# Relative-position bias rows made among the first chunks, 32 copies in DRAM instead of 128, and each Toeplitz tile loaded in four parts

## The chip, the cores and the metric

One core of a Trainium2 chip runs the whole program in one launch. The metric is the device time of that core in microseconds, the median of several runs. A core has five engines that work through their own instruction lists in order and wait for each other by semaphores: TensorE (PE, the matrix products; PEld is its weight load), VectorE (DVE), ScalarE (ACT), GpSimd (POOL) and SyncE (SP). DMA transfers are issued from the lists of SP and of ACT here and carried out by 16 DMA engines.

## The reference

Two transformer blocks on 512 positions of width 1024, in float32. The first block mixes a gated short convolution, a causal attention of 8 heads of 64 with a relative-position bias (with two key blocks of 256 every visible key is taken, so it is plain causal attention), and an attention over 256 memory rows, then a feed-forward part. The second block has an index-based sparse attention, a gated linear recurrence, a memory attention and a feed-forward part. The change lies in the bias of the first block's causal attention:

```
def moba_attention(q, k, v, rel_bias):      # rel_bias: (32 buckets, 8 heads)
    ...
    bias_hb = rel_bias.astype(jnp.float32).T
    ...
        dist = t[:, None] - (own * MOBA_BLOCK + blk_off)[None, :]
        bias_own = bias_hb[:, rel_bucket(dist)]
        s_own = jnp.where(dist[None, None] >= 0, s_own + bias_own[None], NEG)
```

The bias of a head depends on the distance between query and key alone, so one row of 640 numbers per head holds it, with a large negative number where the key lies ahead of the query.

## The kernel before, in words

Every product is made of three float32r products of high and low parts (`passes`, L175 to L177), so each weight tile of 512 KB is loaded by SP (`load`, L187), cast to its high part by ACT (L197) and subtracted to its low part by DVE (L198) ahead of its use. A class `Program` holds the products in the order of TensorE as jobs. Background work is written as Python generators that advance some steps at each tick of the jobs; all of this only sets the order in which instructions stand in each engine's list when the program is built. Nothing is reordered later: an engine that waits holds up all that stands behind it in its list.

The first part of the program runs so. `begin` loads the input, norms the first token tiles, and issues small constant loads from ACT's list (L501 to L503). `head_chunks` makes the first four chunks (q0, k0, q1, k1 of the attention's query and key projections, 128 features each), first for the first 256 positions, then, as half 1, for the other 256; hooks can be put ahead of a (half, chunk). `use_q` and `use_k` copy a finished chunk into operand tiles (`stack_q` L540 and L542, `stack_k` L547 to L551). Then `gemm_N` makes the values v (four weight tiles, copied out at L756). Then come the twelve chunks of the convolution with the remaining q and k chunks between them, and the gate products of the first branch.

The bias is prepared by the generator `bias_rows`, started after the head chunks and driven by the ticks of the v product: it loads a 33x640 one-hot table and the bias table, multiplies them on TensorE (L524, two column parts), copies the 8x640 result from PSUM (L525), and writes each head's row 128 times to a DRAM tile `rdram` [8, 128, 640] (L526). `toeplitz(hd)` then loads a 128x512 tile (L531) from `rdram` with a row step of 639, so that each partition gets the row shifted by one.

```
        nc.scalar.dma_start(rdram, rrow[:, None, :].to_broadcast([8, P, 640]))
        ...
        nc.scalar.dma_start(t, bass.AP(tensor=base.tensor, offset=base.offset + P - 1, ap=[[639, P], [1, 512]]))
```

The attention is the generator `chain(*(moba_pair(c) for c in range(4)))`, at 0.35 step per tick, beside the convolution chunks and the first gates. A pair of heads begins with its two `toeplitz` loads; then `causal_pair` makes the scores of four row blocks i = 3, 2, 1, 0 (`stacked`, L554 and L555); DVE adds the Toeplitz tile and takes the row maximum (L586); ACT makes the exponentials (L588) and, after a reciprocal on DVE (L594), scales them (L597); TensorE transposes them (L307) and multiplies with the values (L614). PSUM has 8 banks (`bank()`), which are taken in turn, so a product can wait for the reader of a bank's former content. The framework also takes the completion semaphores of all DMAs from a small set in turn: a DMA is not issued before the former transfer on its semaphore has landed, whichever list that one was issued from.

Of the kernel before, what the change touches and what calls it, by code (L numbers as in the profile page):

```python
# [28 lines left out]
# columns of the packed per-channel vectors  # L29
# [9 lines left out]
class Program:  # L39
    """The matrix products in the order of the tensor engine, each with the weight tiles it needs.  # L40

    Weight tiles are loaded and split ahead of their use; background work (generators) advances by
    some steps after each product, so that what it waits for is done under the products."""
# [39 lines left out]
    def fetch(self, n):  # L83
        """loads up to n tiles more than are split"""
        while len(self.loaded) < min(len(self.flat), len(self.got) + n):
            self.loaded.append(self.load(self.flat[len(self.loaded)][0]))

    def prepare(self):
        """splits the next tile"""
        self.fetch(1)  # L90
        n = len(self.got)
        kind, on_pool = self.flat[n][1:]
        self.got.append(self.split(self.loaded[n], kind != "w", on_pool))
        self.loaded[n] = None
        self.held += kind == "w"
# [48 lines left out]
def body(tc, ctx, io):  # L144
# [58 lines left out]
    # ---- constants  # L203
# [17 lines left out]
    def rsqrt_small(n, parts, scale, post=None):  # L221
        """(sum * scale + eps) ** -0.5 of [P, n] sums of squares (scale 1 for two partial means)"""
        ms, rs = small(n), small(n)
        if len(parts) == 2:
            g_.tensor_scalar(ms, parts[0], parts[1], EPS, op0=ALU.add, op1=ALU.add)
        else:
            g_.tensor_scalar(ms, parts[0], scale, EPS, op0=ALU.mult, op1=ALU.add)
        g_.tensor_tensor(out=rs, in0=ms, in1=negh[:, :n], op=ALU.pow)  # L228
        if post is not None:
            r2 = small(n)  # L230
            pool_scale(r2, rs, post)
            rs = r2
        return rs
# [6 lines left out]
    class Act:  # L240
        """A [K, tokens] operand, split in two float32r parts, as pairs of 128-row chunks."""
# [16 lines left out]
        def put_pairs(self, j, t, ps, gain=None):  # L258
            """ps: [128, 512] with token tile t of two pairs"""
            parts = []  # L260
            for i in range(2):
                self.alloc(j + i)
                cols = slice(t * P, (t + 1) * P)
                parts.append((self.h[j + i][:, :, cols], self.l[j + i][:, :, cols],
                              ps[:, i * 256:(i + 1) * 256].rearrange("p (k t) -> p k t", k=2)))
            for hi, lo, x in parts:
                if gain is None:
                    a_.copy(hi, x)  # L268
                else:
                    a_.activation(hi, x, AF.Copy, scale=gain)  # L270
            for hi, lo, x in parts:
                if gain is None:
                    sub_lo(lo, x, hi)
                else:
                    v_.scalar_tensor_tensor(lo, x, gain, hi.bitcast(F32), op0=ALU.mult, op1=ALU.subtract)  # L275
# [5 lines left out]
    class Chunks:  # L281
        """A [K, tokens] operand whose 128-row chunks come one by one."""
# [28 lines left out]
    # ---- norms of token tiles  # L311
    def norm_y(x, sq, gain):
        """x: [P, D] of one token tile; sq: its two partial mean squares"""
        rs = rsqrt_small(1, sq, 1.0)
        y = slot([P, D])
        for hf in range(2):
            c = slice(hf * 512, hf * 512 + 512)
            v_.scalar_tensor_tensor(y[:, c], x[:, c], rs, gain[:, c], op0=ALU.mult, op1=ALU.mult)
        return y
# [10 lines left out]
    # ---- products  # L330
    def gemm_T(w, x, out, nk=KD, cols=(0, 512)):
        """out[:, cols] = (weights [nk*128, 128])^T x, in parts; w = (hi, lo) tiles, [k, m] in a row."""
        hi, lo = w
        c0, c1 = cols
        for k in range(nk):
            s = slice(k * P, (k + 1) * P)
            passes(out[:, c0:c1], hi[:, s], lo[:, s], x.hi(k)[:, c0:c1], x.lo(k)[:, c0:c1], k == 0, k == nk - 1)
            if k % 2 and k < nk - 1:
                yield

    def chunk(src, x, use, **kw):
        """job: one 128-feature chunk, feature-major; use(psum)"""
        def f(w):
            o = bank()
            yield from gemm_T(w, x(), o, **kw)
            use(o)
        pr.job(f, [src])

    def head_chunks(srcs, x, uses, before):
        """first chunks of a phase, the first two token tiles ahead of the others;  # L350
        before: hooks {(half, chunk): fn}"""
# [24 lines left out]
    def gemm_N(srcs, x, use, nt=NT):  # L376
        """jobs: a token-major product with one 512-column block; use(t, psum)"""
# [26 lines left out]
    def gemm_out(src, npair, x, epi0, epi1, res=4, korder=None, late=None, need={}):  # L404
        """jobs: [tokens, 1024] = x^T W; src(half, pair) -> DRAM tile; epilogues per token tile.
        late(t) is queued two tiles after epi1(t)."""
# [49 lines left out]
    # ---- the first norm  # L456
# [21 lines left out]
    def begin():  # L478
# [21 lines left out]
        first_norm(2)  # L500
        nc.scalar.dma_start(vecs, io["c_vecs"])  # L501
# [9 lines left out]
    # ---- block 1: relative position bias, as one row per head in DRAM  # L511
    rdram = drp.tile([8, P, 640], F32, name="rdram")

    def bias_rows():
        oneh = slot([33, 640])
        nc.scalar.dma_start(oneh, io["c_onehot"])
        rb = cst.tile([33, 8], F32, name="rb")
        g_.memset(rb[32:33, :], 1.0)
        nc.scalar.dma_start(rb[0:32, :], io["rel_bias"])
        yield from wait(4)  # L520
        rrow = slot([8, 640])
        for c0, c1 in ((0, 512), (512, 640)):
            ps = bank()
            mm(ps[:8, :c1 - c0], rb, oneh[:, c0:c1], start=True, stop=True)  # L524
            v_.tensor_copy(rrow[:, c0:c1], ps[:8, :c1 - c0])  # L525
        nc.scalar.dma_start(rdram, rrow[:, None, :].to_broadcast([8, P, 640]))  # L526

    def toeplitz(hd):
        t = tmp()
        base = rdram[hd]  # L530
        nc.scalar.dma_start(t, bass.AP(tensor=base.tensor, offset=base.offset + P - 1, ap=[[639, P], [1, 512]]))  # L531
        return t

    # ---- attention
    HALVES = ((slice(0, 64), slice(64, 128)), (slice(64, 128), slice(0, 64)))

    def stack_q(dst, ps, scale=1.0):
        """dst: per head [128, n]: the float32r parts of 64 rows, one above the other"""
# [5 lines left out]
    def stack_k(dst, ps):  # L544
        """dst: per head two [128, n]: each of the two parts of 64 rows, twice"""
# [11 lines left out]
    def p_view(sl, s, i):  # L557
        """columns of the triangle's row block i (i + 1 key blocks)"""
# [8 lines left out]
    def causal_pair(ops, vh, addm, put, ready=None):  # L567
        """two heads of 64; ops(s) = stacked (q, kh, kl) of [128, 512]; vh(s, j): [128, 64];
        addm(s, i): [128, (i+1)*128] to add to the scores; put(psum [128, 512])"""
# [47 lines left out]
    def mem_heads(heads, scale, put, parts=False):  # L617
        """heads: (score(t, out), v(j), first row, rows) over 256 memory rows; put(psum [128, 512]);
        v(j) may be the pair of the values' parts"""
# [48 lines left out]
    class MemT:  # L668
        """the normed memory rows, feature-major and split"""
# [35 lines left out]
    # ---- block 1: mixing  # L705
# [52 lines left out]
    def moba_pair(c):  # L758
        def g():
            while ("kl", c) not in qk:  # L760
# [10 lines left out]
                {(0, 1): small_consts, (0, 3): lambda: late_T(2), (1, 0): lambda: late_T(3)})  # L771
    pr.start("bias", bias_rows)
    gemm_N([io["w_in_v"][j] for j in range(4)], H, use_v)
    pr.drain("bias")
# [87 lines left out]
    # ---- norm after a branch, residual, norm before the next one  # L862
    def post_norm(gpost, gpre, half):
        """half: a power of two that the branch's values lack"""
# [35 lines left out]
    def next_head(late, srcs, uses, after=None):  # L900
        """the next phase's first chunks, with the last two tiles' transposes among them"""
# [8 lines left out]
    # ---- block 1: feed forward  # L910
# [32 lines left out]
    # ---- block 2: index scores and the top 128 keys of each query  # L943
# [80 lines left out]
    # ---- block 2: memory attention  # L1024
    def head_norm(ps, nq, nk):
        """ps: [P, (nq + nk) * 64] token-major; rms over 64; the nk last heads come twice each"""
# [20 lines left out]
    def stack_qT(q, t, y, gain):  # L1047
        """the parts of y's four heads of 64, transposed, to q's token tile t"""
# [46 lines left out]
    class Heads:  # L1095
        """four heads' [128, n], in two slots"""
# [47 lines left out]
    # ---- block 2: HGRN2  # L1144
    hg = {}

    def silu2(out, ps):
        """twice silu: x * (1 + tanh(x / 2))"""
# [57 lines left out]
    def hgrn_offsets(j):  # L1206
        """sums of whole 64-chunks between a position's chunk and the level's reference point, of two heads"""
# [16 lines left out]
    class Level:  # L1224
        """one level of one head, in three steps on three engines and the products"""
# [200 lines left out]
    # ---- block 2: the order of the mixing's products  # L1426
# [35 lines left out]
    # ---- block 2: output projection, residual, feed forward  # L1462
# [63 lines left out]
# ---- host side: layouts only  # L1526
def _pack_t(w):
    """[K, M] -> one tile [128 k, (k chunks) 128 m] for each 128 columns"""
# [4 lines left out]
def _pack_n(w, perm=None):  # L1533
    """[K, M] -> tiles [128 k, 2 k chunks, 512 m], the 512-column blocks outermost"""
# [8 lines left out]
def _cols(v):  # L1543
    """[n*128] -> [128, n]"""
    return v.reshape(-1, P).T
# [93 lines left out]
```

## Time and profile before

| what | value |
|---|---|
| time, median of 3 runs | 1602.97 us (1602.64 to 1603.36) |
| profiled execution, first to last instruction | 1605.4 us |
| TensorE busy | 1525.8 us, 95% |
| VectorE, ScalarE, GpSimd busy | 49%, 37%, 15% |
| mean granted TensorE clock | 0.973 |
| DMA, bytes moved | 153.80 MB, mean 96 GB/s |

The page gives for each engine the busy time as a share of the span. The granted clock is told per stretch of time, with 1.00 for full speed. Views by stretch give the busy microseconds of each engine inside it, so the length of the stretch minus PE's busy time is the time in which TensorE had nothing to run. A line of the timeline tells start, duration, engine, line of the program and operation, and in brackets how long the engine was idle before it and what ended the wait; the letter q after an engine's name marks an instruction of its list that only issues a DMA.

### The profile page before, as it was taken

The page shows a single profiled execution, that of the slowest core. Times are in us where ns is not written, and L with a number is a line of the kernel's source. Part 1 is how long each engine was busy: PE and PEld are TensorE (multiplying, and loading weights), DVE is VectorE, ACT ScalarE, POOL GpSimd, SP SyncE. Part 2 cuts the span into 40 slices and gives each one's busy share as a digit, 9 for nine tenths or more (in the row PEclk, how much of TensorE's full clock was granted, in tenths as well). Part 3 has the DMA queues.
Part 4 walks back from the last instruction along what each step waited for, and adds up shares of the span by engine and source line. Part 5 has one row for each costly group of instructions (what it writes and reads, how often), then busy time and mean ns, then how long its engine had stood idle before and what let it go on. Part 6 is the DMA issues. An engine that isn't in the chain of part 4 may idle for free.

```text
span 1605.4 us, 20374 instructions
## 1 busy us (share of the span) xinstructions
PE 1525.8 (95%) x8107; PEld 1265.8 (79%) x8107; DVE 790.3 (49%) x1200; ACT 597.4 (37%) x1043; POOL 238.3 (15%) x344
## 2 busy tenths in 40 slices
PE   8929999999999999999999998999789999999999
PEld 7727788888888888888888986767568988888887
DVE  5215545455345566666324478988744333333231
ACT  5214545344334333333223465465533222222120
POOL 1000000012111100000000167725320000000000
PEclk9959999999999999999999999999799999999999
DMA  5432223332234033223334222221221132232331
GB/s 179 100 62 90 88 90 117 126 98 79 93 112 157 28 104 105 93 92 105 106 118 136 95 89 84 92 72 54 93 79 66 66 103 95 93 104 92 105 118 53
DMA packets 46437, 153.80 MB, mean 96 GB/s; under 512 B 5092, under 2 KB 5604, under 8 KB 46342
## 3 DMA queue, kind: packets, MB, share of 16 engines
q1 hardware_dynamic: 41472, 142.62, 26.9%
q10 hardware_dynamic: 4870, 9.87, 2.8%
q8 instruction: 64, 1.05, 0.3%
q14 instruction: 31, 0.25, 0.0%
HBM read 145.66 MB, written 6.82 MB: 95 GB/s over the span
## 4 chain that ended last, share of the span: by engine, by line
PE 79%; DVE 7%; ACT 4%; POOL 3%; issue 2%; another core or an unknown queue 2%; DMA 1%; SPq 0%; DVEq 0%; POOLq 0%; ACTq 0%
PE p L175 25%; PE p L176 25%; PE p L177 25%; PE p L307 2%; ACT s L588 1%; DVE s L1006 1%; DVE s L1272 1%; POOL m L228 1%; DVE m L1005 1%; ACT t L237 1%; PE p L614 1%; ACT s L597 1%; DVE s L180 0%; POOL s L183 0%
## 5 line engine op out<-in xcount | busy, mean ns | idle before, releaser
L175 PE MATMUL p<-s,wh 128*128 128x512 f32 (+1 forms) x1192 | 465.6, 391 | 0.9 <-DVE t L1312 0.6
L176 PE MATMUL p<-s,wh 128*128 128x512 f32 (+1 forms) x1192 | 462.9, 388 | 0.0
L177 PE MATMUL p<-s,wl 128*128 128x512 f32 (+1 forms) x1192 | 462.5, 388 | 0.0
L198 DVE TENSOR_TENSOR wl<-r,wh 128x1024 fp32r<-128x1024 f32 x217 | 258.3, 1192 | 329.9 <-ACT wh L197 329.0
L197 ACT CAST wh<-r 128x1024 fp32r<-128x1024 f32 x233 | 232.9, 1001 | 232.6 <-PE p L176 220.5
L175 PEld LDWEIGHTS p<-s,wh 128*128 128x128 f32 x1192 | 225.0, 189 | 46.7 <-DVE t L1312 0.8
L177 PEld LDWEIGHTS p<-s,wl 128*128 128x128 f32 x1192 | 225.0, 189 | 45.8
L176 PEld LDWEIGHTS p<-s,wh 128*128 128x128 f32 x1192 | 225.0, 189 | 44.0
L175 PE MATMUL p<-wh,s 128*128 128x512 f32 x544 | 218.5, 402 | 4.4 <-ACT s L270 4.4
L177 PE MATMUL p<-wh,s 128*128 128x512 f32 x544 | 215.0, 395 | 1.1 <-DVE s L275 0.6
L176 PE MATMUL p<-wl,s 128*128 128x512 f32 x544 | 214.6, 394 | 0.0
L176 PE MATMUL p<-s,s 128*128 128x256 f32 (+1 forms) x408 | 132.7, 325 | 5.6 <-DVE s L180 5.6
L175 PE MATMUL p<-s,s 128*128 128x256 f32 (+1 forms) x408 | 133.5, 327 | 0.5 <-ACT s L268 0.5
L177 PE MATMUL p<-s,s 128*128 128x256 f32 (+1 forms) x408 | 132.2, 324 | 0.0
L183 POOL TENSOR_SCALAR s<-t 128x512 fp32r<-128x512 f32 (+1 forms) x64 | 34.7, 543 | 655.7 <-DVE t L930 223.4
L175 PEld LDWEIGHTS p<-wh,s 128*128 128x128 f32 x544 | 103.8, 191 | 26.6 <-ACT s L270 4.8
L177 PEld LDWEIGHTS p<-wh,s 128*128 128x128 f32 x544 | 103.6, 191 | 24.1 <-DVE s L275 1.0
L176 PEld LDWEIGHTS p<-wl,s 128*128 128x128 f32 x544 | 103.9, 191 | 20.2
L176 PEld LDWEIGHTS p<-s,s 128*128 128x128 f32 x408 | 79.9, 196 | 11.9 <-DVE s L180 6.6
L175 PEld LDWEIGHTS p<-s,s 128*128 128x128 f32 x408 | 80.0, 196 | 6.5 <-ACT s L268 1.2
L177 PEld LDWEIGHTS p<-s,s 128*128 128x128 f32 x408 | 79.9, 196 | 5.3
L307 PE MATMUL p<-ident,s 128*128 128x128 f32 x400 | 60.1, 291 | 16.4 <-ACT s L597 6.3
(182 smaller groups left out, 1420.2 us busy)
## 6 DMA issues: line engine op xcount, KB each, us to landing
r<-w_up SPq DMA_DIRECT2D x44, 512.0 KB, 3.4
r<-w_ffn_in SPq DMA_DIRECT2D x44, 512.0 KB, 3.3
r<-w_in_gate SPq DMA_DIRECT2D x24, 512.0 KB, 3.3
r<-w_down SPq DMA_DIRECT2D x22, 512.0 KB, 3.3
r<-w_ffn_out SPq DMA_DIRECT2D x22, 512.0 KB, 3.3
r<-w_out SPq DMA_DIRECT2D x16, 512.0 KB, 3.3
r<-w_in_conv SPq DMA_DIRECT2D x12, 512.0 KB, 3.3
r<-w_in_qk SPq DMA_DIRECT2D x8, 512.0 KB, 3.7
```

Source lines behind the costliest of these rows:

```text
L175: mm(out, sh, mh, start=start, stop=False)
L176: mm(out, sh, ml, start=False, stop=False)
L177: mm(out, sl, mh, start=False, stop=stop)
L183: g_.tensor_scalar(out, x, s, 0.0, op0=ALU.mult, op1=ALU.add)
L197: a_.copy(hi[:, :n], raw)
L198: (g_ if on_pool else v_).tensor_tensor(out=lo[:, :n], in0=raw, in1=hi[:, :n].bitcast(F32), op=ALU.subtract)
L228: g_.tensor_tensor(out=rs, in0=ms, in1=negh[:, :n], op=ALU.pow)
L237: a_.activation(tmp(), x, AF.Square, scale=scale, accum_out=acc)
L307: pe.transpose(ps[:m, n:n + P], s, ident)
L588: a_.activation(pv, pv, AF.Exp, scale=-1.0, bias=negm[s][:, i:i + 1], accum_out=sums[s][:, i:i + 1])
L597: a_.activation(pv, pv, AF.Copy, scale=rec[s][:, i:i + 1])
L614: mm(ps[64 * s:64 * s + 64, j * P:512], vh(s, j), p_view(PT, s, 3 - j), start=(j == 0), stop=(j == 3))
```

## The change

The bias table and one-hot loads go to a new function `bias_load`, called in `begin` ahead of the three constant loads. `bias_rows` is no longer a generator: it is a hook ahead of (half 1, chunk 1), that is between the second halves of q0 and k0. `rdram` holds 32 copies of each row instead of 128, and `toeplitz` loads the 128 partitions in four DMAs of 32 partitions each, every one from the same 32 copies with another offset. Comments and docstrings are emptied besides.

```
     def begin():
...
         first_norm(2)
+        bias_load()
         nc.scalar.dma_start(vecs, io["c_vecs"])
...
-    rdram = drp.tile([8, P, 640], F32, name="rdram")
+    RB = 32
+    rdram = drp.tile([8, RB, 640], F32, name="rdram")
+    rel = {}
+
+    def bias_load():
+        rel["onehot"], rel["rb"] = slot([33, 640]), cst.tile([33, 8], F32, name="rb")
+        g_.memset(rel["rb"][32:33, :], 1.0)
+        nc.scalar.dma_start(rel["rb"][0:32, :], io["rel_bias"])
+        nc.scalar.dma_start(rel["onehot"], io["c_onehot"])
 
     def bias_rows():
-        oneh = slot([33, 640])
-        nc.scalar.dma_start(oneh, io["c_onehot"])
-        rb = cst.tile([33, 8], F32, name="rb")
-        g_.memset(rb[32:33, :], 1.0)
-        nc.scalar.dma_start(rb[0:32, :], io["rel_bias"])
-        yield from wait(4)
         rrow = slot([8, 640])
         for c0, c1 in ((0, 512), (512, 640)):
             ps = bank()
-            mm(ps[:8, :c1 - c0], rb, oneh[:, c0:c1], start=True, stop=True)
+            mm(ps[:8, :c1 - c0], rel["rb"], rel["onehot"][:, c0:c1], start=True, stop=True)
             v_.tensor_copy(rrow[:, c0:c1], ps[:8, :c1 - c0])
-        nc.scalar.dma_start(rdram, rrow[:, None, :].to_broadcast([8, P, 640]))
+        nc.scalar.dma_start(rdram, rrow[:, None, :].to_broadcast([8, RB, 640]))
 
     def toeplitz(hd):
         t = tmp()
         base = rdram[hd]
-        nc.scalar.dma_start(t, bass.AP(tensor=base.tensor, offset=base.offset + P - 1, ap=[[639, P], [1, 512]]))
+        for r in range(0, P, RB):
+            nc.scalar.dma_start(t[r:r + RB, :], bass.AP(tensor=base.tensor, offset=base.offset + P - 1 - r, ap=[[639, RB], [1, 512]]))
         return t
...
     head_chunks([io["w_in_qk"][i] for i in (0, 4, 1, 5)], H, [use_q(0), use_k(0), use_q(1), use_k(1)],
-                {(0, 1): small_consts, (0, 3): lambda: late_T(2), (1, 0): lambda: late_T(3)})
-    pr.start("bias", bias_rows)
+                {(0, 1): small_consts, (0, 3): lambda: late_T(2), (1, 0): lambda: late_T(3), (1, 1): bias_rows})
     gemm_N([io["w_in_v"][j] for j in range(4)], H, use_v)
-    pr.drain("bias")
```

Where the instructions stand now is shown at three places. In the names, `s` is a tile of the large pool, `p` a PSUM bank, `t` one of six 128x512 tiles, `r` a loaded weight tile and `wh` its high part.

ACT's list around the write of `rdram`, before:

```order
L548 CAST s_509<-p_244 64x512
L197 CAST wh_519<-r_227 128x1024
L516 DMA s_535<-c_onehot 33x640
L519 DMA rb<-rel_bias 32x8
L197 CAST wh_558<-r_233 128x1024
L526 DMA rdram<-s_570 1024x1x640
L197 CAST wh_596<-r_239 128x1024
L197 CAST wh_626<-r_523 128x1024
```

The same write in ACT's list now (the two table loads stand ahead of the load of `vecs`, near the list's start):

```order
L268 CAST s_165<-p_389 128x2x128
L544 ACTIVATE s_422<-p_246 64x512 x2
L529 DMA rdram<-s_427 256x1x640
L551 CAST s_459<-p_247 64x512
L552 CAST s_459<-p_247 64x512
```

The write has moved from among the casts of the v weights to the place between the copies of q0 and of k0, and it has a quarter of the rows.

ACT's list at the Toeplitz loads of the first pair, with the semaphores that each instruction waits for, before:

```order
L197 CAST wh_662<-r_562 128x1024 [waits DMAHW1_49,Activation_49]
L531 DMA t_687<-rdram 128x512 [waits DMAHW2_49]
L531 DMA t_689<-rdram 128x512 [waits DMAHW6_49]
L588 ACTIVATE s_703,m_691<-s_703,m_693 128x512 [waits DVE_49]
L588 ACTIVATE s_703,m_692<-s_703,m_694 128x512 [waits DVE_49]
```

And now:

```order
L197 CAST wh_662<-r_570 128x1024 [waits DMAHW2_49,DVE_49]
L535 DMA t_687<-rdram 32x512 [waits DMAHW0_49]
L535 DMA t_687<-rdram 32x512 x3
L535 DMA t_692<-rdram 32x512
L535 DMA t_692<-rdram 32x512 [waits DMAHW3_49]
L535 DMA t_692<-rdram 32x512 [waits DMAHW4_49]
L535 DMA t_692<-rdram 32x512 [waits DMAHW5_49]
L592 ACTIVATE s_709,m_697<-s_709,m_699 128x512 [waits DVE_49]
L592 ACTIVATE s_709,m_698<-s_709,m_700 128x512 [waits DVE_49]
```

Two DMAs have become eight at the same place in the list. The first waits for the write of `rdram` (semaphore 0), the sixth and seventh wait for two weight loads that SP issued earlier (semaphores 3 and 4), and the eighth for the first of the eight, whose semaphore (5) it takes over.

PE's list at the two bias products, before (they stood inside the second v weight tile):

```order
L175 MATMUL p_526<-wh_235,s_152 128x512
L176 MATMUL p_526<-wl_236,s_152 128x512
L177 MATMUL p_526<-wh_235,s_153 128x512
L524 MATMUL p_571<-s_535,rb 8x512
L524 MATMUL p_574<-s_535,rb 8x128
L175 MATMUL p_527<-wh_235,s_152 128x512
```

And now, between the last product of q0 and the first of k0's second half:

```order
L175 MATMUL p_246<-s_165,s_171 128x256
L176 MATMUL p_246<-s_166,s_171 128x256
L177 MATMUL p_246<-s_165,s_172 128x256
L527 MATMUL p_428<-s_210,rb 8x512
L527 MATMUL p_431<-s_210,rb 8x128
L175 MATMUL p_247<-s_150,s_193 128x256
```

The two products have moved ahead by some hundred matmuls; the order of all others on PE is unchanged.

## Prediction, made before the changed kernel ran

> **What bounds the kernel now.** I read the page first. TensorE is busy nearly all of the span, so only stretches without products, or with products at a lower clock, can give time back. The row of granted clocks points at one: the third of the 40 slices, 80 to 120 us, stands at 5 tenths.
>
> ```profile
> span 1605.4 us, 20374 instructions
> PE 1525.8 (95%) x8107; PEld 1265.8 (79%) x8107; DVE 790.3 (49%) x1200; ACT 597.4 (37%) x1043; POOL 238.3 (15%) x344
> PEclk9959999999999999999999999999799999999999
> ```
>
> Then the waits. Of all that TensorE waited for, one wait is by far the longest; in the window around it (47 to 135 us) the chain behind it shows.
>
> ```profile
> PE p L554 <- DVE m L586: 31.5, 2, 30.9
> ...
> DVE s L586 <- DMA t<-rdram: 41.4, 1, 41.4
> ```
>
> The scores (L554) need a PSUM bank that DVE's masked maximum (L586) has to read out first, and that needs its Toeplitz tile. The chain of work that ended last says why the tile was late, and the timeline gives ACT's DMA issues.
>
> ```profile
> 65.68 39.80 another core or an unknown queue
> 105.50 2.71 DMA t<-rdram
> ...
> 49.66 0.80 ACTq L526 DMA_DIRECT2D rdram<-s  x1
> 64.15 0.59 ACT L756 COPY s<-p 128x512 f32<-128x512 f32 x1 [0.77 <-PE p L177]
> 105.50 0.85 ACTq L531 DMA_DIRECT2D t<-rdram  x2
> ...
> DMA to landing us min/median/max: 2.7/2.8/3.4
> ...
> 95.00:100.00 5.00, 0.00 (x0) 0.00 (x0) 0.00 (x0) 0.00 (x0) 0.00 (x0) 0.50 0.47 49
> ```
>
> The write of the bias rows is issued at 49.66, and the first Toeplitz load goes out at 105.50, 55.8 us later, since it must wait for the write; ACT had been done with what stands ahead of it at about 65 us. Alone on the DMA engines the write keeps 0.47 of them busy at 49 GB/s: 128 copies x 8 heads x 2560 bytes = 2.62 MB take 53 us at that rate, and 55.8 with the 2.7 or so of latency that a small load shows. So the unknown queue of the chain is this write. TensorE's stretches then cost this much (columns: length, PE busy, PEld, DVE, ACT, POOL, clock, DMA share, GB/s):
>
> ```profile
> 78.24:109.11 30.87, 0.00 (x0) 0.00 (x1) 0.75 (x3) 0.02 (x1) 0.00 (x0) 0.56 0.47 68
> 109.11:116.28 7.17, 6.51 (x17) 5.19 (x18) 2.85 (x8) 5.37 (x13) 0.00 (x0) 0.50 0.23 73
> 116.28:126.29 10.01, 10.01 (x44) 7.93 (x43) 6.34 (x15) 5.17 (x13) 0.00 (x0) 1.00 0.17 52
> 126.29:128.70 2.41, 0.00 (x1) 0.00 (x0) 0.40 (x3) 1.97 (x5) 0.00 (x0) 1.00 0.00 0
> 129.93:133.35 3.42, 3.42 (x10) 2.65 (x10) 1.89 (x2) 1.47 (x3) 0.00 (x0) 0.50 0.02 5
> ```
>
> **The write of the rows.** It is moved and shortened. It now stands behind the copy of q0 on ACT and waits for DVE's copies of the two bias products. Their rows of before:
>
> ```profile
> 32.33 1.19 ACT L540 ACTIVATE s<-p 64x512 fp32r<-64x512 f32 x2 [3.02 <-PE p L177]
> 33.56 1.39 DVE L542 SCALAR_TENSOR_TENSOR s<-p,s 64x512 fp32r<-64x512 f32 x2 [3.35 <-ACT s L540]
> 47.69 1.24 PE L524 MATMUL p<-s,rb 33*8 33x512 f32 x4
> 48.75 0.88 DVE L525 COPY s<-p 8x512 f32<-8x512 f32 x2 [0.20 <-PE p L524]
> ```
>
> q0 is done on TensorE at 32.3, the bias products end 1.24 later, DVE is free at 34.95 and copies for 0.88: the write is issued at about 35.9. With 32 copies it moves 655 KB, 13.4 us at 49 GB/s, so it has landed near 52 (35.9 + 13.4 + 2.7). The Toeplitz loads can go out at about 64.2, when ACT's list has passed the copy at 64.15. That leaves 12 us of cover: the write could take nearly twice as long and nobody would wait. The weight loads issued beside the write are hurt less too; three loads of 512 KB issued during it landed after 18.4 us in the median:
>
> ```profile
> r<-w_in_conv SPq DMA_DIRECT2D x3, 512.0 KB, 18.4
> ```
>
> That delay cost nothing, since TensorE stood still at the time for another reason. So I count nothing for it either way. The 1.24 us of the bias products are paid in both kernels, at another place.
>
> **The two table loads** move ahead of three constant loads in `begin`, the last of which and the next cast on ACT are these:
>
> ```profile
> 12.83 0.45 ACTq L503 DMA_DIRECT2D lmask<-c_lmask  x1
> 14.68 1.04 ACT L197 CAST s<-r 128x1024 fp32r<-128x1024 f32 x1
> ```
>
> Two more issues of 0.35 end at 14.0, ahead of the cast at 14.68: 0 us. Two of the constant loads now also wait for input loads of SP; should those land later than that, the casts are late by as much, which I bound by the 0.7 us of the two issues. GpSimd's memset moves with them, 0.1 us into idle time: 0.
>
> **The stall at 78 us.** The use of the first tiles, and two Toeplitz loads issued together later on, for the next pair:
>
> ```profile
> 109.03 0.69 DVE L586 CUSTOM_DVE_ANT_0 s<-p,t 128x512 f32<-128x512 f32 x1
> ...
> 149.04 0.81 ACTq L531 DMA_DIRECT2D t<-rdram  x2
> ```
>
> With Toeplitz issues from 64.2 on, each 0.405 us apart (0.81 for two), the eighth goes out at 67.0 and lands 2.8 later, at 69.8. Its tile is used by DVE's second maximum, which in the kernel before started at 109.03, and 19.7 us after that start the transposes ran (128.70, the end of the idle stretch above). They would be ready at 89.5. TensorE gets there from 78.24 with the products of the two rows after the stall, 6.51 us at clock 0.50 (3.26 at full) and 10.01: at 91.5. So it waits neither at 78.24 nor at 126.29, with 2 us to spare. Saved: 30.87 of idle, 0.66 of idle in the next stretch (7.17 - 6.51), 3.25 of half clock, 2.41 of idle, and 1.71 of half clock after it (half of 3.42). That is 38.9 us.
>
> **The four loads per tile.** Eight issues take the place of two in ACT's list for each pair, and the tiles land later. Further rows of pairs 1, 2 and 3, and the later of the two weight loads that pair 1's loads will wait for:
>
> ```profile
> 143.80 0.33 SPq L187 DMA_DIRECT2D r<-w_in_conv  x1
> 153.47 0.69 DVE L586 CUSTOM_DVE_ANT_0 s<-p,t 128x512 f32<-128x512 f32 x1
> 170.37 3.74 ACT L597 ACTIVATE s<-s,m 128x512 f32<-128x512 f32 x8 [1.94 <-DVE m L594]
> 172.35 1.31 PE L307 MATMUL p<-ident,s 128*128 128x128 f32 x10 [0.43 <-ACT s L597]
> ...
> 208.03 3.72 ACT L597 ACTIVATE s<-s,m 128x512 f32<-128x512 f32 x8
> 215.20 1.25 PE L307 MATMUL p<-ident,s 128*128 128x128 f32 x10
> ...
> 250.96 3.74 ACT L597 ACTIVATE s<-s,m 128x512 f32<-128x512 f32 x8 [1.44 <-DVE m L594]
> 257.97 1.25 PE L307 MATMUL p<-ident,s 128*128 128x128 f32 x10
> ```
>
> In pair 1 the eighth load is issued at 149.04 + 7 x 0.405 = 151.9 and lands at 154.7; DVE's second maximum started at 153.47, so all that follows is 1.2 us late, and TensorE already waited 0.43 at the end of that chain: 1.2 us on the path. Pairs 2 and 3 are about as late or later, but there four scaled blocks (half of 3.7 us) are done at 209.9 and 252.8, and TensorE comes for them at 215.2 and 258.0: 5 us of cover, so nothing. How long a load of 32 partitions takes is not in the trace. From below: an issue of 0.33 and the 2.1 us that the 64 KB of `causal` took give a landing at 153.5, cost 0. From above: the 0.80 us issue that the write took, and 2.8, give 157.4, cost 3.9. I take the 0.405 of the loads of the same matrix from the same queue. On semaphores: the sixth, seventh and eighth load of a pair wait for earlier transfers, two for weight loads. In pair 1 the later of those was issued at 143.80, 5 us ahead of the first Toeplitz load, and the eighth waits for the first of its own pair, which lands as its turn comes (149.04 + 2.8 = 151.8): 0.
>
> **A page of the skill on the clock.** The clock fell after short idle times as well:
>
> ```profile
> 891.10:894.52 3.42, 1.59 (x12) 1.24 (x11) 2.74 (x7) 1.32 (x5) 1.96 (x3) 1.00 0.00 0
> 894.52:897.93 3.41, 3.41 (x19) 3.41 (x18) 1.92 (x4) 2.06 (x5) 0.50 (x2) 0.50 0.00 0
> ```
>
> 1.8 us without products in 3.4 were followed by 3.4 us at half clock. Pair 1 would wait 0.43 + 1.2 = 1.6 us, just short of that; if it is 1.8 or more, 1.7 us are added. The Trainium skill (TensorE: Matmul & The Clock Gate, What's actually happening) has the throttle return after at least one idle window of about 3.4 us; by that no wait of 2 us would lower the clock, and the sum would be the same here; the rows above disagree with it.
>
> **The sum.** 38.9 - 1.2 = 37.7 us off the profiled span: 1605.4 becomes 1567.7. The median of the timed runs, 1602.97, lies 2.4 us below that span; 1602.97 - 37.7 = 1565.3.
>
> **Rivals.**
> - *The split loads cost more.* With the upper price in pair 1 (3.9), its half clock (1.7), and pair 0's eighth load at 64.2 + 7 x 0.80 + 2.8 = 72.6, which makes its transposes ready at 92.3 instead of 91.5 (0.8), the gain is 38.9 - 6.4 = 32.5: 1570.5. For it: the queue's issues vary from 0.33 to 0.80 us, and pair 1 has no cover. Against: all loads issued so far stayed at 0.33 to 0.46.
> - *The write does not shrink with its copies*, or its end is not what the loads wait for. Then it still starts 13.8 us earlier (35.9 for 49.66), the loads go out at 91.7, and only 13.8 us are won: 1589.2. For it: what sets its rate, with half of the DMA engines idle, is not in the profile. Against: 2.62 MB at the 49 GB/s of its quiet stretch give its duration.
> - *The loads go one after the other* (slower). If each of a pair's eight loads had to land before the next one moved, a pair would take 8 x 2.8 = 22.4 us instead of 0.4 + 2.8 = 3.2. Pair 0 would be ready at 86.6 and end its chain at 106.3 (22.4 saved instead of 38.9), pair 1 would lose 19.2, pair 2 189.53 + 22.4 - 194.82 - 5.3 = 11.8, pair 3 235.25 + 22.4 - 238.75 - 5.1 = 13.8: 22.4 less, net 22.4 us slower, 1625.4. With L for one load, pair 0 gains 44.8 - 8L, and the others lose 8L - 3.2, 8L - 10.6 and 8L - 8.6, in sum 67.2 - 32L: it decides from L = 2.1 us. The issue times of pairs 2 and 3, and of the maxima there, are in these rows:
>
> ```profile
> 189.53 0.33 ACTq L531 DMA_DIRECT2D t<-rdram  x1
> 194.82 0.69 DVE L586 CUSTOM_DVE_ANT_0 s<-p,t 128x512 f32<-128x512 f32 x1
> 235.25 0.81 ACTq L531 DMA_DIRECT2D t<-rdram  x2
> 238.75 0.69 DVE L586 CUSTOM_DVE_ANT_0 s<-p,t 128x512 f32<-128x512 f32 x1
> ```
>
>   The Trainium skill (DMA: Bandwidth & Descriptors, Rules for kernel authors) speaks for it: transfers to disjoint partition halves serialize, use one transfer of 128 partitions, and under 64 KB it is mostly overhead. Against it: in the row at 149.04 two loads went out within 0.81 us, and no load of these tiles took more than 3.4 from issue to landing; only the eighth waits for one of its own pair.
>
> **How the numbers follow.** Likeliest case 0.78 (gain 35 to 41); dearer split loads 0.14; the write as long as before 0.05; loads in a row 0.03. The predicted time is the first case's, 1565.3. The range takes its bounds and most of the second case: 1561 to 1572. A difference under 0.2%, 3 us, can hardly be told from none; faster 0.96, the same 0.01, slower 0.03.
>
> **What would show it.** In the profile after, the longest wait of L554 on DVE and the half clock in the third slice are gone; the write is issued near 36 and the first Toeplitz load near 64; the transposes of pair 1 wait 1 to 2 us. A Toeplitz load that goes out well after 65, a maximum that waits for its tile by more than 3 us in any pair, or weights that come late between 36 and 64 would prove a step wrong.

## The result and the profile after

| | before | changed |
|---|---|---|
| time, median | 1603.16 us (1602.64 to 1604.94, 4 runs) | 1566.7 us (1565.65 to 1568.02, 4 runs) |
| profiled span | 1605.4 us | 1566.2 us |
| TensorE busy in it | 1525.8 us | 1520.0 us |
| mean granted clock | 0.973 | 0.986 |

The ratio is 0.9771, with a 95% interval of 0.9757 to 0.9785: 36.5 us less. The head of the page, its row of granted clocks, and the DMA packets, for later:

```profile
span 1566.2 us, 20399 instructions
PE 1520.0 (97%) x8107; PEld 1261.1 (81%) x8107; DVE 789.3 (50%) x1200; ACT 597.5 (38%) x1043; POOL 238.3 (15%) x344
PEclk9999999999999999999999999999699999999999
...
DMA packets 46053, 151.83 MB, mean 97 GB/s; under 512 B 5476, under 2 KB 5988, under 8 KB 45958
```

The 5 in the third slice has become a 9. Of the 39.2 us that the span lost, 5.8 are TensorE's busy time (1525.8 less 1520.0, the same 8107 products at a higher clock) and 33.4 its idle time (79.6 to 46.2). The stretches that answer to the stall (columns as before: length, PE, PEld, DVE, ACT, POOL, clock, DMA share, GB/s), the first two of them during the write:

```profile
40.00:45.00 5.00, 5.00 (x37) 4.70 (x36) 4.13 (x6) 2.91 (x6) 0.00 (x0) 1.00 0.48 50
50.00:51.73 1.73, 1.73 (x10) 1.42 (x9) 1.02 (x1) 0.00 (x0) 0.00 (x0) 1.00 0.68 123
70.00:78.24 8.24, 8.24 (x38) 6.90 (x37) 3.34 (x9) 3.82 (x9) 0.00 (x0) 1.00 0.19 59
78.24:90.00 11.76, 11.76 (x57) 9.89 (x56) 6.44 (x15) 6.86 (x17) 0.00 (x0) 1.00 0.22 85
```

The write runs alone at 50 GB/s with 0.48 of the DMA engines, as before, but its last packet is written at 51.7, and TensorE works through the place where it had stood still for 30.87 us. The timeline and the chain of work, in order of time, show the write, the Toeplitz loads, the second maximum of pair 0, its first transposes, and the same for pair 1:

```profile
L529 ACTq DMA_DIRECT2D rdram<-s x1: 797/797/797, 37.0 to 37.0; - x1
...
65.32 0.95 ACTq L535 DMA_DIRECT2D t<-rdram  x2
66.30 2.80 ACTq L535 DMA_DIRECT2D t<-rdram  x6
...
68.67 3.90 DMA t<-rdram
72.73 0.69 DVE L590 CUSTOM_DVE_ANT_0 s<-p,t 128x512 f32<-128x512 f32 x1 [2.27 <-DMA t<-rdram]
...
92.38 1.31 PE L307 MATMUL p<-ident,s 128*128 128x128 f32 x10
...
114.44 2.04 DMA t<-rdram
116.65 0.69 DVE L590 CUSTOM_DVE_ANT_0 s<-p,t 128x512 f32<-128x512 f32 x1 [1.00 <-DMA t<-rdram]
...
135.31 0.88 PE L307 MATMUL p<-ident,s 128*128 128x128 f32 x6 [1.30 <-ACT s L601]
135.31:138.70 3.39, 3.39 (x20) 3.01 (x21) 0.67 (x1) 3.37 (x7) 0.00 (x0) 1.00 0.12 46
```

The row at 92.38 has no bracket: TensorE came to the transposes of pair 0 just as they were ready. In pair 1 the last tile is 1.00 us late for DVE and TensorE waits 1.30; the stretch behind it keeps the full clock.

### The profile page after: what moved, and what is told of

Read it like the earlier page. It is cut to its first block, busy times and chain, and to the rows that moved or that the text cites. A ratio compares the mean times of both kernels' runs of the same rounds, so it can differ in the third digit from the quotient of the medians.

```text
span 1566.2 us, 20399 instructions
## 1 busy us (share of the span) xinstructions
PE 1520.0 (97%) x8107; PEld 1261.1 (81%) x8107; DVE 789.3 (50%) x1200; ACT 597.5 (38%) x1043; POOL 238.3 (15%) x344
## 3 DMA queue, kind: packets, MB, share of 16 engines
q1 hardware_dynamic: 41472, 142.62, 26.6%
## 4 chain that ended last, share of the span: by engine, by line
PE 82%; DVE 7%; ACT 4%; POOL 2%; issue 2%; DMA 2%; ACTq 0%; SPq 0%; DVEq 0%; POOLq 0%
PE p L175 26%; PE p L176 26%; PE p L177 26%; PE p L307 2%; ACT s L592 1%; DVE s L1008 1%; DVE s L1274 1%; DVE m L1007 1%; PE p L618 1%; ACT s L601 1%; POOL m L228 1%; DVE wl L198 1%; DMA s<-mem 0%; POOL s L183 0%; DVE s L180 0%
```

## The experiments

**One part of the change at a time.** The first kernel has only the earlier place, the second only the 32 copies and the four loads.

```
-    RB = 32
+    RB = 128                    # in the changed kernel: one load of 128 partitions
```

> The early place alone: the write of the rows stands where the changed kernel has it, but with 128 copies, and each Toeplitz tile comes in one load. Theory (the first loads wait for the end of the write, which takes 53 us at 49 GB/s wherever it stands): issued at 37.0, last packet near 91.5, first Toeplitz load near 92.0 instead of 105.5; the stall of TensorE at 78 us shrinks from 30.9 to about 18 us, its half clock stays; median 1589 to 1592 us. Rival (the place alone does it, since the write then lies beside other work): no stall at 78 us, 1566 to 1568 us.

Measured: 1592.21 us, ratio 0.9932 (0.9915 to 0.995). The chain around the stall:

```profile
50.75 23.18 DMA r<-w_in_qk
...
75.06 17.70 another core or an unknown queue
92.78 2.68 DMA t<-rdram
...
79.99:96.36 16.37, 0.00 (x0) 0.00 (x0) 0.75 (x3) 0.02 (x1) 0.00 (x0) 0.61 0.49 99
```

The first load goes out at 92.78 and TensorE stands still for 16.4 us: the theory, with a median 0.2 us over its range. Besides, a load of q and k weights needs 23.2 us beside the long write.

```
+    RB = 32                     # in the kernel before, bias_rows unchanged
-        nc.scalar.dma_start(rdram, rrow[:, None, :].to_broadcast([8, P, 640]))
+        nc.scalar.dma_start(rdram, rrow[:, None, :].to_broadcast([8, RB, 640]))
...                              # and the four loads of 32 partitions
```

> The shortening alone: the rows are written where the kernel before writes them, but 32 times, and each tile comes in four loads of 32 partitions. Theory: the write goes out near 49.7, its last packet is written near 65.1, the first Toeplitz load goes out near 65.6, about 1 us after ACT has come to it; TensorE loses up to 1 us before the transposes of the first pair; median 1566 to 1570 us, so nearly the whole gain without the earlier place. Rival (the gain comes from the earlier place): 1590 us or more.

Measured: 1567.47 us, ratio 0.9769 (0.9754 to 0.9785). The write goes out at 49.83, and the first Toeplitz load at 65.18:

```profile
49.83 0.79 ACTq L527 DMA_DIRECT2D rdram<-s  x1
64.32 0.59 ACT L758 COPY s<-p 128x512 f32<-128x512 f32 x1 [0.77 <-PE p L177]
65.18 5.41 ACTq L533 DMA_DIRECT2D t<-rdram  x8
...
92.59 1.31 PE L307 MATMUL p<-ident,s 128*128 128x128 f32 x10 [1.23 <-ACT s L599]
```

That is 0.86 us after ACT's copy ahead of it began; in the changed kernel it was 0.09 (65.32 after 65.23). So the load waited some 0.8 us for the end of the write, about as expected. The eight issues then took 5.41 us instead of 3.78: the seventh waits for a weight load whose semaphore it takes over, and that load, beside the write, took 8.6 us from its issue to its landing instead of 3.2 in the changed kernel. So the shortening alone wins as much as the whole change (ratio 0.9771). Of the earlier place, these two waits are left to see in the trace, as 1.2 us ahead of the transposes of pair 0, and nothing in the time.

**What a longer early write costs.** 64 copies and two loads for each tile:

> The changed kernel with 64 copies and two loads of 64 partitions for each tile. Theory (the write takes 26.5 us, from 38.4 to 65.0, and ACT comes to the loads at 65.3): nobody waits for the write, and the last tile of a pair lands 1.9 us sooner than with four loads; median 1565 to 1567.5 us. Rival (the longer write keeps the weight loads of 37 to 65 us off the engines): weights late, 1569 us or more.

Measured: 1571.3 us (1569.89 to 1573.4), ratio 0.9796 (0.9777 to 0.9814): the rival. The write went out at 38.86 and its last packet was written at 66.9. ACT's timeline, and TensorE at the transposes of pair 0:

```profile
68.67 1.05 ACT L197 CAST wh<-r 128x1024 fp32r<-128x1024 f32 x1 [11.55 <-DMA r<-w_in_qk]
69.74 0.59 ACT L760 COPY s<-p 128x512 f32<-128x512 f32 x1
69.97 0.51 ACTq L535 DMA_DIRECT2D t<-rdram  x1
...
96.84 2.39 PE L307 MATMUL p<-ident,s 128*128 128x128 f32 x10 [2.62 <-ACT s L601]
96.84:100.30 3.46, 3.46 (x14) 3.19 (x15) 0.73 (x1) 2.69 (x5) 0.00 (x0) 0.51 0.02 5
```

A weight load was late by the write, ACT waited 11.55 us for it, and the copies of v and the Toeplitz loads stand behind that cast in ACT's list. The next weight load took 16.9 us from its issue to its landing; the same load took 4.6 in the changed kernel. TensorE lost 2.62 us and a stretch at half clock. In this execution, the slowest of the four, the write also started 1.9 us later than in the changed kernel: ACT had waited 2.84 us for a load of v weights at 23 us, and TensorE 2.03 us at 27.7, ahead of the write. So 1.9 of the 5.4 us by which its span is longer (1571.6 for 1566.2) are not the weight load's, and of the 4.6 us between the medians the share is not known.

**The price of the split loads.** One load for each tile, from 35 copies:

```
-    RB = 32
+    RB = 35
-        for r in range(0, P, RB):
-            nc.scalar.dma_start(t[r:r + RB, :], ... base.offset + P - 1 - r, ap=[[639, RB], [1, 512]])
+        nc.scalar.dma_start(t, ... base.offset + P - 1, ap=[[608, 4], [639, 32], [1, 512]])
```

> The changed kernel, but with 35 copies instead of 32 and one load of 128 partitions for each tile (partition 32r+s reads from copy r+s, so that all strides are positive). Theory (the four loads cost what pair 1 waits more): the tiles of pair 1 land 2 us sooner, TensorE's wait ahead of its transposes falls from 1.30 to about 0.4 us; median 1565.0 to 1566.5 us, 0.2 to 1.3 us under the changed kernel. Rival (the split costs nothing that can be seen): the wait stays near 1.3 us and the time at 1566.7. Rival (one load of four runs is dearer than four): slower than 1567.5.

Measured: 1578.78 us (1575.76 to 1582.46), ratio 0.9845 (0.9826 to 0.9864): slower than four loads, the last rival, and far beyond its bound of 1567.5. The DMA packets of its page, the chain at the loads of pair 0, and TensorE's waits in pair 0 and pair 1:

```profile
DMA packets 45597, 151.89 MB, mean 97 GB/s; under 512 B 4996, under 2 KB 5508, under 8 KB 45502
...
65.25 9.02 DMA t<-rdram
...
94.06 1.31 PE L307 MATMUL p<-ident,s 128*128 128x128 f32 x10 [2.44 <-ACT s L600]
...
129.30 0.47 PE L175 MATMUL p<-s,wh 128*128 128x512 f32 x1 [3.14 <-DVE s L554]
```

The second load takes 9.0 us from its issue; one load of a tile takes 2.6 to 2.9 in the last kernel of this section. There are 480 packets under 512 bytes fewer than in the changed kernel: 32 loads with 16 completions each make 512, 8 loads with 4 each make 32. So such a load ran on 4 DMA engines instead of 16. The Trainium skill (DMA: Bandwidth & Descriptors, Why a DMA increments its semaphore by 16 and not by 1) has the slowest dimension of the access pattern set the number of engines; the outer dimension here is 4, and the trace agrees. The experiment priced another thing than it was made for. Its profiled execution is the fastest of the four, with a span 7.8 us over the changed kernel's, so the 12.1 us between the medians are not all in the trace.

Twice as many loads, 16 copies with eight loads for each tile:

> The changed kernel with 16 copies and eight loads of 16 partitions for each tile: 16 issues for a pair in place of 8. Theory (each issue puts the last tile 0.47 us later, and pairs 0 and 1 have no cover): the last load of pair 0 lands near 76, 3.8 us later than in the changed kernel, so TensorE waits some 3.5 us ahead of the first transposes, and 5 us instead of 1.3 in pair 1; each of the two waits brings one stretch of 3.4 us at half clock (1.7 us); pairs 2 and 3 have 5 us of cover; median 1574 to 1580 us. Rival (the number of loads costs nothing): 1566 to 1568 us.

Measured: 1584.44 us (1581.54 to 1586.33), ratio 0.9873 (0.9849 to 0.9897): the direction of the theory, 4 us beyond its range. ACT's issues of pair 0, the chain in both pairs, and stretches at and behind the waits:

```profile
66.11 8.55 ACTq L535 DMA_DIRECT2D t<-rdram  x14
...
67.90 3.61 DMA r<-w_in_conv
...
96.12 2.39 PE L307 MATMUL p<-ident,s 128*128 128x128 f32 x10 [4.00 <-ACT s L601]
96.12:99.50 3.38, 3.38 (x13) 3.18 (x14) 0.65 (x1) 2.70 (x5) 0.00 (x0) 0.50 0.03 5
120.93 3.69 DMA r<-w_in_conv
127.62 1.94 DMA t<-rdram
...
126.00:136.96 10.96, 5.41 (x24) 3.94 (x23) 3.57 (x7) 3.95 (x8) 0.00 (x0) 0.76 0.07 15
136.96:140.40 3.44, 3.44 (x8) 2.79 (x9) 1.61 (x5) 2.24 (x5) 0.00 (x0) 0.50 0.00 0
```

The wait of pair 0 is 4.00 us (3.5 expected), but that is partly luck: the tenth issue stood 2.2 us behind the ninth, waiting for the weight load issued at 67.90, whose semaphore it takes over, and the last load landed 1.9 us after its issue, where the changed kernel's took 3.9. In pair 1 the eleventh issue waits for a weight load on the semaphore that it takes over (the chain runs through `w_in_conv` there), and TensorE loses 5.55 us in the window of 10.96 (1.95 and 3.60) with clock lost in both of the last two rows: busy time rises by 7.4 us in all (1527.4 against 1520.0), where the expectation had two stretches, 3.4 us.

**What sets the rate of the write.** The kernel before, with its 128 copies at their place, but other source partitions for the rows of the bias. The edit of the first of four kernels (`rbw` holds the bias table with each head's column 16 times, so that the product gives each row on 16 partitions):

```
-            mm(ps[:8, :c1 - c0], rb, oneh[:, c0:c1], start=True, stop=True)
+            mm(ps[:, :c1 - c0], rbw.rearrange("p h r -> p (h r)"), oneh[:, c0:c1], start=True, stop=True)
-        nc.scalar.dma_start(rdram, rrow[:, None, :].to_broadcast([8, P, 640]))
+        nc.scalar.dma_start(rdram.rearrange("h (r c) x -> (h r) c x", c=8), rrow[:, None, :].to_broadcast([P, 8, 640]))
```

> The kernel before with its 128 copies at their place, but the bias product gives each row on 16 partitions (128 instead of 8), and each partition is written 8 times. Theory (8 source partitions let only 8 DMA engines work, at 392 ns a packet of 2560 bytes): 16 engines work, the write takes about 27 us and ends near 79, the first Toeplitz load goes out near 79.5, the stall at 78 us falls from 30.9 to 5 us or so; median 1575 to 1581 us. Rival (the rate of 49 GB/s is that of the written memory, not of the source): nothing changes, 1602 to 1604 us. If the packets get faster too (100 ns, as the first ones took), the write ends before 65 and the time is 1565 to 1568 us.

> The kernel before with 128 copies at their place, each row on 2 partitions (16 in all) that are written 64 times each. Theory A (a packet takes 392 ns wherever an engine reads one partition only): 16 engines, 64 packets each, 25 us; the write ends near 76, the first Toeplitz load goes out near 76.5, TensorE loses 2 us at 78 and some 6 us ahead of the first transposes, median 1572 to 1578 us. Theory B (8 engines at work were the limit, with 16 the packets take 107 ns): the write ends near 59, median 1565.5 to 1568 us.

In the other two the write is that of the kernel before, from `rrow[0:32:4]` and `rrow[0:16:2]`:

> The kernel before, with 128 copies at their place from 8 source partitions as before, but these are every fourth partition (0, 4, ... 28) instead of 0 to 7. Theory P (four neighbouring partitions share one way out of the on-chip memory, about 26 GB/s: 4 packets of 2560 bytes at a time in 392 ns): each of the 8 engines has a way of its own, a packet takes about 107 ns as with 128 partitions, the write takes 14 us and ends near 66; median 1565.5 to 1569 us. Theory A (a packet takes 392 ns as long as an engine reads one partition only): the write ends near 105 as before, 1601 to 1605 us. The Trainium skill (SBUF, State Buffer: Door 1, the DMA port swizzle) has four neighbouring partitions on one port of about 27 GB/s; by that it is theory P.

> The same with every second partition (0, 2, ... 14). Theory P: two engines share a way, a packet takes about 196 ns, the write takes 25 us and ends near 77, as in the kernel with 16 neighbouring partitions; median 1574 to 1580 us. Theory A: 392 ns, the write ends near 105, 1601 to 1605 us.

Measured: 1566.94 us with 128 partitions (0.9772, 0.9757 to 0.9786), 1578.71 with 16 (0.9838, 0.9819 to 0.9857), 1567.23 with every fourth (0.9764, 0.9703 to 0.9825), 1576.86 with every second (0.9824, 0.976 to 0.9889). The same stretch of each, during the write and ahead of the next weight load:

128 partitions:

```profile
53.00:55.50 2.50, 2.50 (x13) 2.07 (x12) 0.00 (x0) 0.95 (x1) 0.00 (x0) 1.00 1.02 392
```

16 neighbouring partitions:

```profile
53.00:55.50 2.50, 2.50 (x13) 2.07 (x12) 0.89 (x1) 1.05 (x1) 0.00 (x0) 1.00 0.91 98
```

Every fourth of 32:

```profile
53.00:55.50 2.50, 2.50 (x12) 2.06 (x11) 0.97 (x1) 1.05 (x1) 0.00 (x0) 1.00 0.52 207
```

Every second of 16:

```profile
53.00:55.50 2.50, 2.50 (x11) 2.01 (x10) 0.00 (x0) 0.54 (x1) 0.00 (x0) 0.85 0.47 99
```

The first kernel came out as the third case of its expectation: the packets got faster too. The second, 0.7 us over the range of its theory A, refutes B. On the last two A and P differ, and both came out in the range of P. The last column is the rate, the one ahead of it the share of the 16 DMA engines. With 16 neighbouring partitions twice as many engines are busy as with 8 (0.91 and 0.47) and the rate is twice 49. With 8 partitions at steps of 1, 2 and 4 the share stays about one half, and the rate is 49, 99 and 207. So with few groups neither the engines nor the number of partitions set it, but how many groups of four neighbouring partitions are read: 2, 4 and 4 groups give 49, 98 and 99 GB/s, some 25 for each. With 8 groups the rate is still 26 for each (207), but there, as with all partitions (392), an engine at work also moves some 25 GB/s (207 over 0.52 of 16 engines, 392 over 16), so those two rows do not tell which of the two holds the rate. Theory P holds, theory A falls. The Trainium skill (SBUF, State Buffer: Door 1, the DMA port swizzle) has each group of four on one of 16 ports of about 27 GB/s, and the rows with 2 and 4 groups agree. With all of 128 partitions the write is so short that 128 copies at the old place and one load for each tile are as fast as the changed kernel.

**A version with what was learned**: the early place, 128 copies from 128 partitions, one load for each tile.

> The early place of the changed kernel, with 128 copies that are written from 128 partitions, and one load for each tile. Theory (a load of 128 partitions over 16 engines lands 2.5 us after its issue, and the write of 7.5 us has long ended): no wait at 78 and 91 us, TensorE waits 0.43 us instead of 1.30 ahead of the transposes of pair 1; median 1564.5 to 1566.5 us, 0.5 to 1.5 us under the changed kernel. Rival (nothing is left to win, other waits take it): 1566.7 as the changed kernel.

Measured: 1565.83 us (1564.47 to 1569.15), ratio 0.9764 (0.9743 to 0.9784). TensorE's idle time from 30 to 330 us falls from 1.75 us in the changed kernel to 0.81, with 0.43 instead of 1.30 in pair 1 and nothing at 78 and 91 us. The time can't be told from the changed kernel's; that it is faster is not shown.

## Why the prediction was right, point by point

- *The time*: 1565.3 predicted, 1566.7 measured. On the span, 37.7 us were predicted and 39.2 came: 32.7 and 33.4 of idle time, 5.0 and 5.8 of clock. That the length of the write is the cause is shown by the second kernel above, and by the one with every fourth partition, where the write differs in its source partitions alone; that the loads wait for its end is shown by the first.
- *The write*: predicted from 35.9 to 52. It went out at 37.0, since TensorE was 0.65 us later at 12 us and 1.1 us later from 21 us on. The 0.65 come from an input tile that came later, ahead of anything that was changed (its norm on ACT, before and after); the rest arose where full clock is recorded from 17.3 us before and from 19.0 after:

```profile
7.35 0.63 ACT L237 ACTIVATE t<-s 128x512 f32<-128x512 f32 x1 [0.84 <-DMA s<-x]
```

```profile
8.00 0.63 ACT L237 ACTIVATE t<-s 128x512 f32<-128x512 f32 x1 [1.86 <-DMA s<-x]
```

  Its packets took 13.3 us for 13.4 predicted. The rival of a write that does not shrink is refuted.
- *The cover of the write*: "the write could take nearly twice as long and nobody would wait" does not hold. With 64 copies it took 26.6 us, a little over that, and ACT waited 11.55 us for a weight load issued beside it, whose cast stands ahead of the Toeplitz loads in the same list: they went out at 69.97 instead of 65.32, 1.9 us of it by the late start. The step that failed is the one on the weight loads: their 18 us were counted at nothing, because in the kernel before they fell into the stall. With 32 copies the count came out right, since the write ended at 51.7.
- *The stall*: gone, with all five terms. The 2 us to spare at pair 0 were not there: the first load went out 1.1 later than said (65.3 for 64.2), the eighth 0.5 more (an issue takes 0.47, not 0.405), and it landed after 3.9 us instead of 2.8, so it came 2.8 us late, and TensorE itself was at the transposes some 0.8 later than said. That no wait came there was luck, to within a tenth of a microsecond: the late write of 32 copies left 1.23 us at the same place.
- *Pair 1*: 1.6 us of wait predicted, 1.30 measured. The issues were dearer, but the small loads landed sooner, after 1.9 us in the median for 2.8. No half clock followed, as forecast for a wait under 1.8 us.
- *Loads in a row* (the slower rival, L from 2.1 us on): refuted. The eight loads went out 0.47 us apart in both pairs. In pair 1 the last landed 5.2 us after the first issue (111.26 to 116.48), where a row of 1.9 us each would have taken 15; in pair 0 it was 7.3 us. The split has its price all the same: it costs pair 1 some 0.9 us (1.30 against 0.43 in the last kernel), and twice the loads cost 17.7 in the medians.

## What to carry to other kernels

A wait of 30 us on a DRAM round trip was ended by making the write shorter than the time until its reader comes; once it is, starting earlier adds nothing that can be measured. Before a broadcast write is cut or moved, look at its rate: a source on 8 neighbouring partitions gave 49 GB/s, the same 8 rows on every fourth partition 207. And a slow write must not be counted as free because it has time: what is loaded beside it, and stands ahead of its reader in the same list, is late with it.

## What the runs showed of the hardware

- DMA reads of on-chip memory: some 25 GB/s for each group of four neighbouring partitions that is read, shown with 2 groups (49, on 8 DMA engines) and with 4 (99 on 8 engines, 98 on 16). With 8 groups on 8 engines (207) and all groups on 16 (392) each engine moves some 25 GB/s, too, and which of the two limits is open.
- A load whose access pattern has 4 as its outer dimension ran on 4 DMA engines, and two tiles had landed 9.0 us after the second issue; four loads of 32 partitions each ran on 16.
- The half clock does not follow from the length of one wait. In each profile the clock changes only at the borders of stretches of 3.41 us that lie on one grid (in the kernel before, for example, at 82.14, 116.28, 129.93 and 133.35 us, which are 10, 4 and 1 such stretches apart), and nearly always the idle time inside one stretch decided. Of the 2.41 us ahead of the transposes before, 2.18 lay in the stretch ahead of the half clock:

```profile
126.52:129.93 3.41, 1.23 (x11) 1.23 (x12) 0.18 (x2) 3.20 (x7) 0.00 (x0) 1.00 0.00 0
```

  In the kernel with one load for each tile, 2.44 us fell into two stretches, with 0.66 and 1.77 us idle, and the full clock stayed; of its 3.14 us in pair 1, 2.88 fell into one, and half clock followed:

```profile
88.87:92.28 3.41, 2.75 (x13) 1.94 (x11) 2.99 (x6) 0.30 (x2) 0.00 (x0) 1.00 0.00 0
92.28:95.70 3.42, 1.65 (x13) 1.56 (x14) 0.00 (x0) 3.42 (x8) 0.00 (x0) 1.00 0.00 0
95.70:99.11 3.41, 3.41 (x17) 2.79 (x16) 1.92 (x2) 1.39 (x3) 0.00 (x0) 1.00 0.06 14
126.42:129.83 3.41, 0.53 (x2) 0.48 (x3) 3.34 (x7) 0.04 (x1) 0.00 (x0) 1.00 0.00 0
129.83:133.25 3.42, 3.42 (x10) 2.64 (x9) 1.59 (x4) 2.19 (x5) 0.00 (x0) 0.50 0.00 0
```

  Over the twelve profiles, 69 stretches at full clock had 1.79 us or more without products, and half clock followed every one; of the other 5220, six were followed by it, with 0.98 to 1.70 us. So idle time is not all that counts; what else does was not tried. The smallest is the 0.98 us of the kernel with every second partition, in a stretch that holds the products of the bias; the 0.85 in its row above comes from it.
